# A two-layer diffusion backbone on one core: first norm by VectorE's sum with filling products on TensorE, and a last feed-forward with a late rstd, tokens on partitions and its gate in the weights

## The chip, the core and the metric

The kernel runs on one core of a Trainium2 chip. The core has five engines, each with its own in-order instruction stream: TensorE (PE in the profile, its weight loads PEld), VectorE (DVE), ScalarE (ACT), GpSimd (POOL) and SyncE (SP). SP's stream here holds only DMA issues; its queue is called SPq. Products land in PSUM, which has eight banks of 128 x 512 f32. The metric is device time in microseconds, the median over runs of the whole program. Lower is better.

## The reference

The program computes two layers on 256 latent tokens and 256 context tokens of width 1024. `x` and `ctx` share all weights and have conditioning vectors of their own. Each layer is a feed-forward, a mixer and a second feed-forward, each behind a norm with adaLN (`mx`, `mc`: shift, scale, gate):

```python
mx = jnp.split((cond_x @ mod_w[layer] + mod_b[layer])[:, None, :], N_MOD, axis=-1)
x = x + 0.5 * mx[2] * swiglu(modulate(rms_norm(x, norm_g[layer, 0]), mx[0], mx[1]),
                             ffn_w_in[layer, 0], ffn_w_out[layer, 0])
hx = modulate(rms_norm(x, norm_g[layer, 1]), mx[3], mx[4])
...
x = x + mx[5] * ox
x = x + 0.5 * mx[8] * swiglu(modulate(rms_norm(x, norm_g[layer, 2]), mx[6], mx[7]),
                             ffn_w_in[layer, 1], ffn_w_out[layer, 1])
...
return rms_norm(x, final_norm_g)
```

The mixer that makes `ox` is latent attention in layer 0 and windowed grouped attention in layer 1. The context goes the same way, but not behind the last layer's mixer. `rms_norm(x, g)` is x times the reciprocal root of the mean square of its 1024 values (the rstd), times g; `modulate(h, shift, scale)` is h * (1 + scale) + shift; `swiglu` splits h @ w_in in two halves of 2816, takes silu(first) * second and multiplies by w_out.

## The kernel before

**Layout.** Activations lie with features on the 128 partitions: x is eight tiles (d = 0 to 7) of 128 x 512, the first 256 columns latent tokens (`X`), the rest context (`C`). A matrix product in f32 is made of three products of rounded parts: `split` writes a high half (ScalarE, L182 or L185) and a low half, the rest (VectorE or GpSimd, L183 or L186), and `mm3` (L205) multiplies high by high, high by low and low by high (L210, L211, L212). Weights arrive as 128 x 1024 blocks through `weight` (L194): a load on SP's queue into one of three `wraw` slots, a cast to `whi` and a difference to `wlo`, four slots each.

**Order.** A planner orders each engine's stream by the program's order and by when it takes operands to be ready; `behind(ins)` (L163) puts instructions behind another on its engine. DMAs on SP's queue stay in program order, and an issue that waits for its slot holds all behind it.

**The start.** SP issues four constants, then the eight tiles of x (L76), then for each of the eight feature columns k the adaLN weights of its shift and scale (`load_column`, L114: 1 MB in four loads) and, behind columns 0, 1, 3 and 5, one block of w_in (`lead_weight`, L849). ScalarE squares x (L839), and TensorE sums the squares with a 128 x 128 matrix of ones in plain f32 (L840), which leaves the sum on all partitions; a root and a reciprocal over 128 x 256 follow for each stream (L857, L858). Per column, `mod_on_pe` (L124) multiplies the adaLN weights by the conditioning vectors (L128), copies, transposes (L133) and adds bias and gain per stream on VectorE (L138 to L140); `inputs` (L860) makes the column's scaled, shifted, split input (L863, L865, L866); `lead_products` (L870) multiplies the blocks present so far with the columns present so far.

**Feed-forward.** `ffn` (L410) walks 22 tiles f of 128 hidden features. For each it takes the first product's two halves (`products`, L334: 24 products each), evicts silu(gate) * up as a split pair, and `pump`s (L169) `per_tile` steps of the background. After each of three groups of 8, 7 and 7 tiles, `closing` (L367) multiplies the group by w_out, eight strips of 128 output features, and adds gate times product to x (`residual`, L361). On the last group, `closing` also collects the next norm's squares (`grown`, L266), loads the next sub-layer's first weights (`prefetch`, L310), makes the rstd (`rstd_of`, L217), then the inputs (`stream`, L285), then the first products (`leading`, L317).

**Background.** The other adaLN rows are a matrix-vector product on VectorE: `mod_in_background` (L142) loads eight 128 x 1024 blocks (two `modraw` slots, SP's queue) and adds each into an accumulator per stream (L149, L151), then sums over partitions on TensorE (L157) and transposes.

**The end.** The windowed attention's `closing` leads to the last feed-forward, which has the latent stream alone, so its products are 256 columns wide. Behind it `Final` (L347) scales x by rstd and gain and stores eight strips of features. Its last program lines are:

```python
    sl, nxt = nxt, Sublayer(1, 2, (0,), ffn_specs(1, 1)[:2])
    swa(sl, nxt)
    ffn(nxt, Final(1, 3, (0,), ()))
```

## Time and profile before

| what | us |
|---|---|
| median of 3 runs | 1713.83 (1713.79 to 1716.16) |
| the profiled execution's own time | 1715.96 |
| its span | 1714.2 |
| busy TensorE in the span | 1674.9 (98%) |
| busy VectorE / ScalarE / GpSimd | 1029.5 / 643.9 / 175.2 |
| first 16 us: busy TensorE | 10.07 |
| 16 to 36 us: busy TensorE, granted clock | 15.43, 0.83 |
| 36 to 60 us: busy TensorE | 21.81 |
| 230 to 400 us (inside a feed-forward): busy TensorE | 170.00 |
| 1503 to 1515 us (ahead of the last feed-forward): busy TensorE, granted clock | 7.61, 0.72 |
| 1702.35 to the end: busy TensorE | 1.64 |

How to read the views: a group's row has line, engine, operation, tiles and shapes, count, then busy time and mean ns of one, then idle time of the engine just before and what ended it. A row in order of time begins with start and length in us. A row by stretch has begin and end, length, the busy time of PE, PEld, VectorE, ScalarE and GpSimd with instruction counts, the granted TensorE clock (1.00 is full), the share of the DMA engines and GB/s. Records of matmuls overlap, so the rate of products is read from the distance of their starts, not from a record's length.

### The profile page before, as it was taken

The numbers are of one execution on the slowest core, as the hardware profiler recorded it, in microseconds if no ns is written. First come the engines' busy times: TensorE is split into PE (matmuls) and PEld (weight loads), VectorE is DVE, ScalarE is ACT, GpSimd is POOL, SyncE is SP. The second block draws the span as 40 slices with busy tenths as digits, with TensorE's granted clock in tenths as the row PEclk, the third lists the DMA queues.
The fourth block names the chain that finished last, engine by engine and source line by source line (L and its number), as shares of the span: only waits on it lengthen the run. The fifth ranks groups of instructions, "written<-read, shape, count | busy, mean of one in ns | idle before, by whom it ended". The sixth has DMA issues, their size and how long they took to land.

```text
span 1714.2 us, 23757 instructions
## 1 busy us (share of the span) xinstructions
PE 1674.9 (98%) x9448; PEld 1421.5 (83%) x9448; DVE 1029.5 (60%) x1536; ACT 643.9 (38%) x1087; POOL 175.2 (10%) x173
## 2 busy tenths in 40 slices
PE   7999999999999999999999999999999999989997
PEld 4788888888888898888888898888888897789997
DVE  4877477555568567856857465645433467655554
ACT  4432232224456444213222353223222367554443
POOL 1000000004132040000000130000000352110001
PEclk9999999999999999999999999999999999999998
DMA  9556356442211126644645336734332222145553
GB/s 340 174 192 209 112 198 194 138 132 80 87 50 62 47 68 206 202 158 147 208 145 172 111 111 197 240 117 154 104 101 90 93 90 84 60 149 184 172 188 98
DMA packets 72831, 242.71 MB, mean 142 GB/s; under 512 B 8848, under 2 KB 10640, under 8 KB 72720
## 3 DMA queue, kind: packets, MB, share of 16 engines
q1 hardware_dynamic: 72720, 241.20, 43.1%
q8 instruction: 74, 1.21, 0.3%
q14 instruction: 37, 0.30, 0.1%
HBM read 240.11 MB, written 1.05 MB: 141 GB/s over the span
## 4 chain that ended last, share of the span: by engine, by line
PE 90%; DVE 3%; ACT 3%; DMA 2%; issue 2%; POOL 1%; SPq 0%; POOLq 0%; ACTq 0%; DVEq 0%
PE bank L210 28%; PE bank L211 28%; PE bank L212 28%; DMA r2k<-in_modo 1%; PE bank L157 1%; DVE wlo L183 1%; DVE small L451 0%; PE bank L479 0%; ACT whi L182 0%; PE bank L223 0%; PE bank L102 0%; PE bank L800 0%; ACT tmp L457 0%; DVE r2k L294 0%; DMA big<-in_win 0%
## 5 line engine op out<-in xcount | busy, mean ns | idle before, releaser
L210 PE MATMUL bank<-r2k,whi 128*128 128x512 f32 (+1 forms) x2610 | 916.0, 352 | 4.7 <-ACT r2k L185 2.4
L212 PE MATMUL bank<-r2k,wlo 128*128 128x512 f32 (+1 forms) x2610 | 912.0, 350 | 4.3 <-POOL wlo L183 2.2
L211 PE MATMUL bank<-r2k,whi 128*128 128x512 f32 (+1 forms) x2610 | 913.0, 350 | 2.9 <-DVE r2k L186 1.2
L182 ACT CAST whi<-wraw 128x1024 fp32r<-128x1024 f32 (+1 forms) x313 | 321.6, 1028 | 892.0 <-PE bank L211 537.7
L210 PEld LDWEIGHTS bank<-r2k,whi 128*128 128x128 f32 x2610 | 493.5, 190 | 84.1 <-ACT whi L182 9.2
L212 PEld LDWEIGHTS bank<-r2k,wlo 128*128 128x128 f32 x2610 | 495.1, 190 | 69.7 <-POOL wlo L183 3.1
L211 PEld LDWEIGHTS bank<-r2k,whi 128*128 128x128 f32 x2610 | 495.2, 190 | 68.2 <-DVE r2k L186 1.9
L183 DVE TENSOR_TENSOR wlo<-wraw,whi 128x1024 fp32r<-128x1024 f32 (+1 forms) x302 | 363.6, 1206 | 145.5 <-ACT whi L182 138.8
L151 DVE SCALAR_TENSOR_TENSOR big<-modraw,conds,big 128x1024 f32<-128x1024 f32 x196 | 242.4, 1279 | 12.4 <-DMA modraw<-in_modw 11.9
L248 POOL TENSOR_TENSOR strip<-strip 128x256 f32<-128x256 f32 x64 | 65.7, 1040 | 1319.9 <-issue 657.5
L364 DVE SCALAR_TENSOR_TENSOR x<-bank,mod,x 128x256 f32<-128x256 f32 x192 | 86.1, 480 | 181.9 <-PE bank L212 181.9
L425 DVE TENSOR_TENSOR tmp<-bank,tmp 128x512 f32<-128x512 f32 (+1 forms) x88 | 54.9, 624 | 179.9 <-PE bank L212 178.0
L183 DVE TENSOR_TENSOR r2k<-tmp,r2k 128x512 fp32r<-128x512 f32 (+1 forms) x88 | 54.4, 618 | 1.5 <-ACT r2k L182 1.4
L182 ACT CAST r2k<-tmp 128x512 fp32r<-128x512 f32 (+1 forms) x88 | 49.7, 566 | 10.8 <-DVE tmp L425 10.5
L183 DVE TENSOR_TENSOR r2k<-bank,r2k 128x512 fp32r<-128x512 f32 (+2 forms) x73 | 40.7, 593 | 17.5 <-ACT r2k L182 17.1
L423 ACT ACTIVATE tmp<-bank 128x512 f32<-128x512 f32 (+1 forms) x88 | 47.3, 537 | 7.4 <-PE bank L212 7.4
L451 DVE TENSOR_REDUCE small<-bank 128x1 f32<-128x512 f32 (+1 forms) x64 | 37.0, 614 | 7.4 <-PE bank L774 7.2
L182 ACT CAST r2k<-bank 128x512 fp32r<-128x512 f32 (+2 forms) x73 | 34.4, 524 | 14.2 <-PE bank L212 8.8
L242 ACT ACTIVATE strip<-x 128x256 f32<-128x256 f32 x80 | 30.6, 410 | 17.8 <-DVE x L364 17.0
L186 DVE SCALAR_TENSOR_TENSOR r2k<-r2k,mod 128x256 fp32r<-128x256 f32 x45 | 29.3, 674 | 8.4 <-ACT r2k L185 7.9
L457 ACT ACTIVATE tmp<-bank,small 128x512 f32<-128x512 f32 x32 | 21.8, 687 | 24.8 <-DVE small L453 14.6
L104 DVE TENSOR_TENSOR mod<-bank,c_modb 128x4 f32<-128x4 f32 x56 | 5.3, 154 | 37.2 <-PE bank L102 37.2
(156 smaller groups left out, 933.1 us busy)
## 6 DMA issues: line engine op xcount, KB each, us to landing
wraw<-in_win SPq DMA_DIRECT2D x172, 512.0 KB, 3.5
modraw<-in_modw SPq DMA_DIRECT2D x128, 512.0 KB, 4.2
wraw<-in_wout SPq DMA_DIRECT2D x64, 448.0 KB, 3.3
wraw<-in_wout SPq DMA_DIRECT2D x32, 512.0 KB, 3.8
r2k<-in_modo SPq DMA_DIRECT2D x32, 256.0 KB, 5.8
wraw<-in_mwo SPq DMA_DIRECT2D x8, 512.0 KB, 3.5
wraw<-in_swq SPq DMA_DIRECT2D x8, 512.0 KB, 3.4
wraw<-in_swo SPq DMA_DIRECT2D x8, 512.0 KB, 3.5
```

Source lines behind the costliest of these rows:

```text
L151: nc.vector.scalar_tensor_tensor(acc[s], raw, conds[:, kt, s:s + 1], acc[s], ALU.mult, ALU.add)
L182: nc.scalar.copy(hi, src)
L183: return engine.tensor_tensor(lo, src, hi.bitcast(F32), ALU.subtract)
L210: nc.tensor.matmul(o, lhsT=ah, rhs=bh, start=(i == 0), stop=False)
L211: nc.tensor.matmul(o, lhsT=ah, rhs=bl, start=False, stop=False)
L212: nc.tensor.matmul(o, lhsT=al, rhs=bh, start=False, stop=(i == n - 1))
L242: nc.scalar.activation(q, x, AF.Square)
L248: nc.gpsimd.tensor_tensor(self.parts[0], self.parts[0], q, ALU.add)
L364: nc.vector.scalar_tensor_tensor(xs[d][:, SL[s]], o[:, SL[s]], mod[l][:, s, c:c + 1], xs[d][:, SL[s]], ALU.mult, ALU.add)
L423: nc.scalar.activation(sg[:, :w], og[:, :w], AF.Silu)
L425: nc.vector.tensor_tensor(pr[:, :w], ou[:, :w], sg[:, :w], ALU.mult)
L451: nc.vector.tensor_reduce(top[:, j:j + 1], o[:, :w], axis=AX.X, op=ALU.max)
```

## The change

At the start: the four constants go out on ScalarE's queue, and x comes as four loads of two tiles. The squares are added up on VectorE; four narrow products with a column of ones give the sums by token on partitions, root and reciprocal run over four columns, and four transposes spread the result over partitions again. Column 0's adaLN products come ahead of that in the program. TensorE gets products of ones that nobody reads (`fill`): 40 from the beginning, 3 and 5 behind the first two columns' transposes. The bias and gain steps do both streams in one instruction. The low halves of the four lead weights move from GpSimd to VectorE. In the first feed-forward (`late=2`) the background starts at tile 2, and tiles 12 to 15 take three steps instead of two.

At the end: a class `Raw` takes the place of the last norm. Its first product runs on gain times x, without the rstd, with two more columns that hold the shift; the eviction multiplies by the rstd and adds the shift's product. `last_ffn` makes the second product with tokens on partitions and 512 output features as columns, added up over all 22 tiles in four PSUM banks; the gate (made as a row on all partitions in the background) is multiplied into w_out by GpSimd, and x is added to the sums by products with the identity. The final norm is done from PSUM, and the output is stored token by token. The rest of the program is as before, apart from the layout of x, of w_out and of the output, and a smaller scratch for software DMAs, which the program doesn't use.

```diff
-    cond_raw = load_const("cond", (P, KT, 2))
-    ident = load_const("ident", (P, P))
-    modb = load_const("modb", (P, 2, 72))
-    ng = load_const("ng", (P, 2, 3, KT))
+    cond_raw = load_const("cond", (P, KT, 2), queue=nc.scalar)
+    ident = load_const("ident", (P, P), queue=nc.scalar)
+    modb = load_const("modb", (P, 2, 72), queue=nc.scalar)
+    ng = load_const("ng", (P, 2, 3, KT), queue=nc.scalar)
     x_all = const.tile([P, KT, TT], F32, name="x")
     xs = [x_all[:, d] for d in range(KT)]
-    for d in range(KT):
-        nc.sync.dma_start(xs[d], t["xT"][d])
+    for d in range(0, KT, 2):
+        nc.sync.dma_start(x_all[:, d:d + 2], t["xT"][:, d:d + 2])
...
+    def fill(n, after=None):
+        b = bank()
+        with behind(after):
+            for _ in range(n):
+                nc.tensor.matmul(b[:, :P], lhsT=ones, rhs=ones, start=True, stop=True)
...
+    fill(40)
...
+    def mod_on_pe(k, psA, n=0, after=None):
         sA = tmp()[:, :P]
         nc.scalar.copy(sA, psA[:, :P])
         psB = bank()[:, :P]
-        nc.tensor.transpose(psB, sA, ident)
+        turned = nc.tensor.transpose(psB, sA, ident)
+        if n:
+            fill(n, turned)
         vB = psB.rearrange("p (c i r) -> p c i r", c=2, i=2)
-        for s in range(2):
-            v = mod[0][:, s, :2 * KT].rearrange("p (c k) -> p c k", c=2)[:, :, k]
-            bias = modb[:, 0, :2 * KT].rearrange("p (c k) -> p c k", c=2)[:, :, k]
-            nc.vector.tensor_tensor(v, vB[:, :, 0, s], bias, ALU.add)
-            nc.vector.tensor_tensor(v, vB[:, :, 1, s], v, ALU.add)
-            nc.vector.scalar_tensor_tensor(coefA[0][:, s, 0, k:k + 1], v[:, 1:2], 1.0, ng[:, 0, 0, k:k + 1], ALU.add, ALU.mult)
+        v = mod[0][:, :, :2 * KT].rearrange("p s (c k) -> p c s k", c=2)[:, :, :, k]
+        bias = modb[:, 0, :2 * KT].rearrange("p (c k) -> p c k", c=2)[:, :, k:k + 1].to_broadcast([P, 2, 2])
+        with behind(after):
+            nc.vector.tensor_tensor(v, vB[:, :, 0, 0:2], bias, ALU.add)
+        nc.vector.tensor_tensor(v, vB[:, :, 1, 0:2], v, ALU.add)
+        nc.vector.scalar_tensor_tensor(coefA[0][:, :, 0, k], v[:, 1], 1.0, ng[:, 0, 0, k:k + 1].to_broadcast([P, 2]), ALU.add, ALU.mult)
...
+                n = 0 if f < late else per_tile + (6 * late <= f < 8 * late)
...
+    class Raw(Sublayer):
+        W = T + 2
+        def grown(self, s, d):
+            x = xs[d][:, X]
+            zh, zl = r2k(self.W), r2k(self.W)
+            nc.scalar.activation(zh[:, :T], x, AF.Identity, scale=self.gain(0, d))
+            nc.vector.scalar_tensor_tensor(zl[:, :T], x, self.gain(0, d), zh[:, :T].bitcast(F32), ALU.mult, ALU.subtract)
+            shift = self.shift(0, d).to_broadcast([P, 2])
+            nc.scalar.copy(zh[:, T:], shift)
+            nc.gpsimd.tensor_tensor(zl[:, T:], shift, zh[:, T:].bitcast(F32), ALU.subtract)
+            self.hs.append((zh, zl))
+            self.squares[s].add(x)
+        def terms(self, w, M, cols=None):
+            return [(pair(w, slice(None), slice(k * M, (k + 1) * M)), self.hs[k]) for k in range(KT)]
+        def stream(self, s):
+            pass
+        def leading(self, s):
+            for k in range(KT):
+                for wt, o, M in self.lead:
+                    mm3(o[:M, :self.W], self.terms(wt, M), (k,))
+            _, self.r = self.rstd(s)
...
+        for half in range(2):
+            cols = slice(half * 512, half * 512 + 512)
+            b = bank()
+            nc.tensor.matmul(b, lhsT=ones, rhs=acc[:, cols], start=True, stop=True)
+            nc.vector.tensor_tensor(gate[:, cols], b, gate[:, cols], ALU.add)
+            yield
+        nc.gpsimd.tensor_scalar_mul(gate, gate, 0.5)
...
+        acc = [[bank() for _ in range(2)] for _ in range(2)]
+        r = sl.r
+        held = []
+        def second(f, gu, w):
+            for i in range(2):
+                rows = slice(i * P, (i + 1) * P)
+                for h in range(2):
+                    cols = slice(h * 512, h * 512 + 512)
+                    for j, (a, b) in enumerate(((0, 0), (0, 1), (1, 0))):
+                        nc.tensor.matmul(acc[i][h], lhsT=gu[a][:, rows], rhs=w[b][:, cols],
+                                         start=(f == 0 and j == 0), stop=(f == NF - 1 and j == 2))
+        for f in range(NF):
+            og, ou = next(outs), next(outs)
+            raw = weight_raw(t["woutn"][f])
+            nc.gpsimd.tensor_tensor(raw, raw, gate, ALU.mult)
+            wt = weight_split(raw)
+            while held and f != NF - 2:
+                second(*held.pop(0))
+            ends = small(2)
+            nc.scalar.copy(ends[:, 0:1], og[:, T:T + 1])
+            nc.scalar.copy(ends[:, 1:2], ou[:, T:T + 1])
+            g, u = tmp(T), tmp(T)
+            nc.vector.tensor_tensor(g, og[:, X], r, ALU.mult)
+            nc.scalar.activation(g, g, AF.Silu, bias=ends[:, 0:1])
+            nc.vector.tensor_tensor(u, ou[:, X], r, ALU.mult)
+            nc.vector.scalar_tensor_tensor(u, u, ends[:, 1:2], g, ALU.add, ALU.mult)
+            gu = (r2k(T), r2k(T))
+            hi = nc.scalar.copy(gu[0], u)
+            nc.vector.tensor_tensor(gu[1], u, gu[0].bitcast(F32), ALU.subtract)
+            held.append((f, gu, wt))
+            if f in (5, 7, 9, 11):
+                i, h = (f - 5) // 4, (f - 5) // 2 % 2
+                for d in range(4):
+                    nc.tensor.matmul(acc[i][h][:, d * P:(d + 1) * P], lhsT=xs[4 * h + d][:, i * P:(i + 1) * P], rhs=ident,
+                                     start=False, stop=False)
+        with behind(hi):
+            nc.scalar.activation(small(1), r[:, 0:1], AF.Sqrt)
+        second(*held.pop())
+        for i in range(2):
+            sums, rs = small(2), small(1)
+            ys = [tmp() for _ in range(2)]
+            for h in range(2):
+                nc.scalar.activation(ys[h], acc[i][h], AF.Square, accum_out=sums[:, h:h + 1])
+            nc.vector.tensor_tensor(rs, sums[:, 0:1], sums[:, 1:2], ALU.add)
+            nc.scalar.activation(rs, rs, AF.Sqrt, scale=1.0 / D, bias=eps)
+            nc.vector.reciprocal(rs, rs)
+            for h, queue in enumerate((nc.sync, nc.scalar)):
+                cols = slice(h * 512, h * 512 + 512)
+                if i == 0 and h == 1:
+                    nc.scalar.activation(ys[h], acc[i][h], AF.Copy, scale=rs)
+                    nc.gpsimd.tensor_tensor(ys[h], ys[h], fngr[:, cols], ALU.mult)
+                else:
+                    nc.vector.scalar_tensor_tensor(ys[h], acc[i][h], rs, fngr[:, cols], ALU.mult, ALU.mult)
+                queue.dma_start(out[i, :, cols], ys[h])
...
+        if squares is None:
+            squares = q
+        else:
+            nc.vector.tensor_tensor(squares, squares, q, ALU.add)
     load_table(AF.Sqrt, q)
+    total = bank()
+    for j in range(4):
+        nc.tensor.matmul(total[:, j:j + 1], lhsT=squares[:, j * P:(j + 1) * P], rhs=ones[:, 0:1], start=True, stop=True)
...
+    sums0 = mod_sums(raws[0])
+    root = small()
+    nc.scalar.activation(root, total[:, 0:4], AF.Sqrt, scale=1.0 / D, bias=eps)
+    nc.vector.reciprocal(root, root)
+    wide = bank()
+    for j in range(4):
+        nc.tensor.transpose(wide[:, j * P:(j + 1) * P], root[:, j:j + 1].to_broadcast([P, P]), ident)
+    rstds = [strip() for _ in range(2)]
+    for r, cols in zip(rstds, SL):
+        nc.scalar.copy(r, wide[:, cols])
     def lead_weight(after=None):
         with behind(after):
-            wt = weight_split(wraws[len(sl.lead)], nc.gpsimd)
+            wt = weight_split(wraws[len(sl.lead)])
...
-    mod_on_pe(0, raws[0])
+    mod_on_pe(0, sums0, 3)
     inputs(0)
     for k in range(1, KT + 1):
         if k < KT:
-            mod_on_pe(k, raws[k])
+            mod_on_pe(k, mod_sums(raws[k]), 5 if k == 1 else 0, sl.end if k == 1 else None)
...
-    ffn(sl, nxt, 2)
+    ffn(sl, nxt, 2, 2)
...
-    background.extend(mod_in_background(1, c, (0,)) for c in range(5, 9))
+    background.extend(mod_in_background(1, c, (0,)) for c in range(5, 8))
+    background.append(mod_row_in_background(8))
...
-    sl, nxt = nxt, Sublayer(1, 2, (0,), ffn_specs(1, 1)[:2])
+    sl, nxt = nxt, Raw(1, 2, (0,), ffn_specs(1, 1)[:2])
     swa(sl, nxt)
-    ffn(nxt, Final(1, 3, (0,), ()))
+    last_ffn(nxt)
```

More of the change, by code (lines that the diff above doesn't have):

```diff
@@ L429, in ffn @@
             last = g == len(GROUPS) - 1
-            closing([(t[f"wout{g}"][l, which, d], gu) for d in range(KT)], 2 + 6 * which, l, streams,
+            closing([(t[f"wout{g}"][2 * l + which, d], gu) for d in range(KT)], 2 + 6 * which, l, streams,
                     nxt if last else None, 2 if last else 0, per_tile // 2)
@@ L827, in swa, with products @@
         closing([(t["swo"][d], O) for d in range(KT)], 5, l, (0,), nxt, 0)
+    class Raw(Sublayer):
[19 more added lines that the diff above has]
+            _, self.r = self.rstd(s)
+        def products(self, specs):
+            for i, (ap, size) in enumerate(specs):
+                if i < len(self.lead):
+                    yield self.lead[i][1]
+                else:
+                    wt = weight(ap, size)
+                    o = bank()
+                    mm3(o[:, :self.W], self.terms(wt, P))
+                    yield o
@@ new lines, in mod_row_in_background @@
+    def mod_row_in_background(c):
+        nc.sync.dma_start(gate, t["gater"])
+        acc = big().bitcast(F32)[:, :1024]
+        for kt in range(KT):
+            raw = ring.tile([P, 1024], F32, tag="modraw", name="modraw", bufs=2)
+            nc.sync.dma_start(raw, t["modw"][1, c, kt])
+            if kt == 0:
+                nc.vector.tensor_scalar_mul(acc, raw, conds[:, kt, 0:1])
+            else:
+                nc.vector.scalar_tensor_tensor(acc, raw, conds[:, kt, 0:1], acc, ALU.mult, ALU.add)
+            yield
[4 more added lines that the diff above has]
+            nc.vector.tensor_tensor(gate[:, cols], b, gate[:, cols], ALU.add)
+            yield
+        nc.gpsimd.tensor_scalar_mul(gate, gate, 0.5)
@@ L835, in hybrid_backbone_kernel @@
     sl = Sublayer(0, 0, (0, 1), ffn_specs(0, 0)[:4])
-    total = bank()
+    squares = None
     for d in range(KT):
@@ L1005 @@
     got = r.results[0]["out_x"]
[L1006 removed]
+    return np.ascontiguousarray(got.reshape(1, T, D))
```

56 lines of the change are left out of this document (24 added, 32 removed).

## The prediction

> **What bounds the kernel now.** I read the page's engine shares first, then the busy time by stretch, then the order of time inside the two stretches in which TensorE is not full.
>
> ```profile
> span 1714.2 us, 23757 instructions
> PE 1674.9 (98%) x9448; PEld 1421.5 (83%) x9448; DVE 1029.5 (60%) x1536; ACT 643.9 (38%) x1087; POOL 175.2 (10%) x173
> ```
>
> ```profile
> 16.00:36.00 20.00, 15.43 (x190) 10.44 (x191) 13.01 (x43) 8.84 (x18) 5.50 (x3) 0.83 1.05 402
> 36.00:60.00 24.00, 21.81 (x174) 15.61 (x172) 15.33 (x45) 7.80 (x16) 3.94 (x2) 1.00 0.41 141
> ...
> 1503.00:1515.00 12.00, 7.61 (x44) 7.03 (x43) 7.41 (x13) 8.06 (x17) 4.99 (x7) 0.72 0.27 89
> 1516.60:1702.35 185.75, 185.67 (x1543) 185.06 (x1542) 104.02 (x131) 82.04 (x116) 6.04 (x6) 1.00 0.52 168
> 1702.35:1714.20 11.85, 1.64 (x11) 1.07 (x9) 3.78 (x7) 3.95 (x8) 2.31 (x3) 0.61 0.25 89
> ```
>
> Columns: stretch, length, busy PE, PEld, DVE, ACT, POOL (with instructions), granted clock, DMA share, GB/s. TensorE bounds the span, so time is to be had only where it idles, runs at a low clock, or does work that can go. The change touches such places: the first 60 us, the 13.7 us ahead of the last feed-forward's steady part, that part (185.75 us, full), and the 11.85 us behind its last product.
>
> The start, in order of time (start, length, engine, line):
>
> ```profile
> 2.58 3.75 SPq L76 DMA_DIRECT2D x<-in_xT  x8
> 5.93 10.05 PE L840 MATMUL bank<-tmp,ones 128*128 128x512 f32 x16 [5.93 <-ACT tmp L839]
> 8.17 3.99 ACT L839 ACTIVATE tmp<-x 128x512 f32<-128x512 f32 x6 [1.25 <-DMA x<-in_xT]
> 16.52 3.37 DVE L858 RECIPROCAL strip<-strip 128x256 f32<-128x256 f32 x2 [12.94 <-ACT strip L857]
> 20.34 0.48 DVE L863 SCALAR_TENSOR_TENSOR strip<-x,coefA,strip 128x256 f32<-128x256 f32 x1
> 24.79 1.94 PE L128 MATMUL bank<-r2k,cond 128*32 128x128 f32 x32
> 26.66 0.80 PE L210 MATMUL bank<-r2k,whi 128*128 128x512 f32 x1
> 30.08 1.08 PE L128 MATMUL bank<-r2k,cond 128*32 128x128 f32 x32
> 34.09 1.04 ACT L182 CAST whi<-big 128x1024 fp32r<-128x1024 f32 x1
> 35.20 2.37 POOL L183 TENSOR_TENSOR wlo<-big,whi 128x1024 fp32r<-128x1024 f32 x1 [8.50 <-DMA r2k<-in_modo]
> 36.26 1.33 DVE L140 SCALAR_TENSOR_TENSOR coefA<-mod,c_ng 128x1 f32<-128x1 f32 x1
> 38.03 0.15 DVE L140 SCALAR_TENSOR_TENSOR coefA<-mod,c_ng 128x1 f32<-128x1 f32 x1
> 45.28 2.36 POOL L183 TENSOR_TENSOR wlo<-big,whi 128x1024 fp32r<-128x1024 f32 x1 [7.70 <-ACT whi L182]
> 48.03 0.39 PE L210 MATMUL bank<-r2k,whi 128*128 128x512 f32 x1
> 52.14 0.39 PE L212 MATMUL bank<-r2k,wlo 128*128 128x512 f32 x1
> 58.40 2.48 DVE L151 SCALAR_TENSOR_TENSOR big<-modraw,conds,big 128x1024 f32<-128x1024 f32 x2
> 60.79 1.22 DVE L183 TENSOR_TENSOR wlo<-wraw,whi 128x1024 fp32r<-128x1024 f32 x1
> 62.07 0.50 PE L212 MATMUL bank<-r2k,wlo 128*128 128x512 f32 x1 [1.97 <-DVE wlo L183]
> ```
>
> The reciprocal over 128x256 twice holds the first input back to 20.34. TensorE then runs cold (0.80 at 26.66 for a product that takes 0.39 at 48.03), and each of the four lead weights waits for a cast behind the inputs and 2.36 us of GpSimd. After the leads it stands idle for 1.97 us until 62.07, because a weight's low half queues on VectorE behind two adaLN steps (58.40 to 60.88).
>
> The last feed-forward:
>
> ```profile
> 1502.89 0.28 PE L212 MATMUL bank<-r2k,wlo 128*128 128x256 f32 x1
> 1516.54 0.28 PE L211 MATMUL bank<-r2k,whi 128*128 128x256 f32 x1
> 1702.07 0.28 PE L212 MATMUL bank<-r2k,wlo 128*128 128x256 f32 x1
> 1710.85 1.02 SPq L359 DMA_DIRECT2D out_x<-strip  x2
> ```
>
> **The start, worked out.** Constants leave SP's queue, so x starts about 1.8 us earlier (2.58 to 0.74 at best) and the loads behind it as much; the last square ends at 10.3 instead of 12.16. Seven adds on VectorE follow at 618 ns each (row below), the last about 11.1. The forty filling products are plain f32 of 128 columns: the 16 L840 records took 10.05 us for 8 products of 512, mostly cold, so 40 of a quarter the width cost at most 12.5 us and end between 10 and 13; I take 12.6. Then the four sums and column 0's adaLN products (1.1), square root and reciprocal over four columns (0.4 together), four transposes, two copies (0.4 each): rstd near 15.3 and the first input at 15.7, 4.6 us earlier than 20.34. The clock then stays up: the adaLN products at 24.79 take 1.08 for 1.94 (-0.9), and the nine products between 26.66 and 30.08 take 9 x 0.228 = 2.05 for 3.4 (-1.35); 0.228 is 4.11 us over the 18 products from 48.03 to 52.14. So the third weight's cast moves from 34.09 to about 27.3 (-6.8). Its low half costs 1.22 on VectorE instead of 2.37 (-1.1), the fourth's again (-1.1), and TensorE finds less high-half work to do meanwhile (+0.5): the leads end 8.5 us earlier. Behind them no adaLN step is issued for two tiles, SP does not stand on their loads, and the stall to 62.07 shrinks to about 0.1: -1.9. Sum -10.4. The adaLN steps come back as a third one per tile in tiles 12 to 15. There VectorE has 3 x 2 x 1.28 for them (L151's mean on the page) plus 2.44 for two weights and 1.3 for products and split, 11.4 us in a tile of 48 x 0.228 = 10.9: 2 us too much over four tiles, inside what three weights ahead cover; I charge +0.5, 3 if the cover is gone, and +0.3 for the gate row's wider sums on TensorE. Bounds of the start: -3 (the earlier loads and one shorter low half) to -13 (TensorE's own work, 96 x 0.228 + 8 x 1.1 + 1.8 of filling, without a gap from 13 us).
>
> ```profile
> L183 DVE TENSOR_TENSOR r2k<-tmp,r2k 128x512 fp32r<-128x512 f32 (+1 forms) x88 | 54.4, 618 | 1.5 <-ACT r2k L182 1.4
> L151 DVE SCALAR_TENSOR_TENSOR big<-modraw,conds,big 128x1024 f32<-128x1024 f32 x196 | 242.4, 1279 | 12.4 <-DMA modraw<-in_modw 11.9
> ```
>
> [...]
>
> **The last feed-forward, worked out.** These rows price its parts (mean ns in the middle):
>
> ```profile
> L183 DVE TENSOR_TENSOR wlo<-wraw,whi 128x1024 fp32r<-128x1024 f32 x49 | 60.0, 1225 | 40.2 <-ACT whi L182 40.2
> L182 ACT CAST whi<-wraw 128x1024 fp32r<-128x1024 f32 x49 | 51.4, 1049 | 75.3 <-PE bank L211 37.6 <-issue 35.4 <-PE bank L212 1.5
> L425 DVE TENSOR_TENSOR tmp<-bank,tmp 128x256 f32<-128x256 f32 x22 | 9.3, 424 | 16.0 <-PE bank L212 15.6 <-ACT tmp L423 0.5
> ...
> L457 ACT ACTIVATE tmp<-bank,small 128x512 f32<-128x512 f32 x32 | 21.8, 687 | 24.8 <-DVE small L453 14.6
> wraw<-in_win SPq DMA_DIRECT2D x37, 512.0 KB, 3.5
> 1390.87 1.02 PE L739 MATMUL bank<-tmp,permr 128*128 128x256 f32 x4
> 1391.73 1.03 PE L739 MATMUL bank<-r2k,permr 128*128 128x256 f32 x4
> ```
>
> Before, from 1503.0 (end of the attention's products): 13.7 us to the steady part at 1516.6, 185.75 us of 1536 products (0.1209 each), 11.85 us of tail: 211.2. After: the 48 lead products need no rstd, so they follow at once, the first 42 covering the last strip's residual, gain and split: 48 x 0.121 = 5.8. Sums and transposes of the rstd still pass TensorE: 1.2. The other 1008 products have 258 columns; between 0.1209 at 256 and 0.228 at 512 a straight line gives 0.1217: 122.7 us (bounds 121.9 and, at the price of 512, 230). The second product is 264 of 512 instead of 528 of 256: 60.2 us for 63.8. The residual enters as 16 plain f32 products of 128 columns: two of 256 took 0.86 us at L739, so 0.215 each, 3.4; unhidden weight loads could make it 9; I take 3.8. Waits at entry and in the last two tiles, where two second products are kept back to cover the last eviction: 1. The tail: four squares at 0.69 and some 0.2 for the accumulated sum, the first two under the last products; then add, root, reciprocal (0.6), two scalings from PSUM (0.7 each), and a DMA like the last before (issue 1710.85, end 1714.2: 3.3 for two): about 7. Sum 201.7, that is -9.5 (bounds -13 and, waits of 0.3 a tile and a 9 us residual, +2).
>
> Per tile TensorE needs 48 x 0.1217 + 12 x 0.228 = 8.6 us. VectorE has 3 x 1.225 + 4 x 0.42 = 5.4, ScalarE about 4.3, GpSimd the gating of one weight, 2.36 by the rows of the low halves. None is the bound, but the gated weight's way round its slot is long: 3.5 load + 2.36 + 1.05 + 1.23 + handovers 0.4 = 8.5. It is used a tile and a half after its cast, which covers delays. The new gains and splits in the attention's closing (about half a microsecond a strip on ScalarE and on VectorE, beside a cast and a low half, against 24 x 0.12 = 2.9 us of products) are hidden there.
>
> The row at 36.26 speaks against the gating: a 128x1 step, 0.15 at 38.03, lasted 1.33 until GpSimd's 2.37 had ended. [...]
>
> **Sum.** -10.4 + 0.8 - 9.5 = -19.1. The profiled execution took 1715.96 with a span of 1714.2, so 1696.9 in its terms; it stands 2.1 above the median of 1713.83, so the median should be about 1695.
>
> **Rivals.**
> *Only the end gains.* The start stays tied to the columns' loads, which run at 402 GB/s from 16 to 36 us, and VectorE, now with 4 x 1.22 of low halves among its inputs, is late for each weight: -3 there, 1703. For it: DMA share 1.05. Against: from 36 us the share falls to 0.41 and TensorE still has 24 us to go.
> *The start reaches TensorE's floor*, the planner filling gaps: -13 there, 1692 with the rest, 1689 if the tail is shorter too. Against: the order of weights, each behind inputs 1, 3, 5.
> *The gated weight sets the pace.* If GpSimd and VectorE block each other by one operation each (+1.2), the slot's round is 9.7; it exceeds 8.6 by 1.1, over 21 tiles 23 us less a cover of 12: +11, 1706.
> *Slower.* One mechanism: that round grows to 11 us, VectorE's two SBUF inputs waiting 2.4 for the gating and GpSimd's 1.2 for them in every tile. Then (11 - 8.6) x 21 - 12 = +38: 1733. It decides from a round of 10.1 on, where 31 - 12 eats the 19 gained. For it: 36.26. Against: slots and casts run ahead of need by more than a tile.
> *It does not do what it says:* 258 columns fall out of the fast rate. At the price of 512 that is +108: 1803. No row has such a width; a straight line is likelier.
>
> **How the numbers follow.** Forecast 0.56 (own range 1689 to 1701), only the end 0.13, the floor 0.11, the paced end 0.10, slower 0.06, slow width 0.02, a return to the old time 0.02. Eight in ten lie from 1686 to 1711. About 0.2% (3.4 us) is what a measurement here tells from no change. Faster: 0.56 + 0.13 + 0.11 + 0.10 = 0.90; same 0.02; slower 0.08.
>
> **What would show it.** Right: first input near 16, clock full from 16 to 36, leads ended 8 us earlier, no stall behind them, lead products of the last feed-forward dense from the attention's last one on, tiles of 8.6 us, tail near 7. Wrong: low halves of the leads later than 30 and 39; waits of TensorE on low halves or gated weights in every tile; the 258-wide product above 0.125 apart; filling still running after 14 us.

## The result and the profile after

| | median us | ratio to the kernel before | 95% interval |
|---|---|---|---|
| before, in the same rounds | 1714.38 (1713.79 to 1716.16) | 1 | |
| after | 1700.76 (1699.09 to 1701.59) | 0.9916 | 0.9904 to 0.9929 |

The change made the kernel 13.6 us faster; 19.1 were forecast. The profiled execution of after took 1699.09 us with a span of 1697.3, 16.9 less than the span before. The other 3.3 us of the difference to 13.6 come from the two profiled executions: that of before stood 1.6 above its median, that of after 1.7 below. The run without gating further down had one execution at a granted clock of 0.752 (2062.65 us), which its figures leave out.

The shares of after, and busy time by stretch (columns as in the prediction: length, busy PE, PEld, DVE, ACT, POOL, granted clock, DMA share, GB/s):

```profile
PE 1672.6 (99%) x9294; PEld 1417.5 (84%) x9294; DVE 1080.8 (64%) x1538; ACT 645.4 (38%) x1132; POOL 222.5 (13%) x186
```

```profile
16.00:36.00 20.00, 18.51 (x214) 12.97 (x209) 14.07 (x35) 8.16 (x18) 0.00 (x0) 1.00 1.04 384
36.00:60.00 24.00, 24.00 (x160) 18.48 (x159) 15.42 (x32) 12.61 (x21) 0.00 (x0) 1.00 0.58 200
...
1490.76:1496.56 5.80, 5.80 (x50) 5.80 (x49) 2.61 (x5) 3.53 (x6) 2.84 (x4) 1.00 0.79 244
1496.56:1509.88 13.32, 10.20 (x72) 9.13 (x71) 10.02 (x13) 7.55 (x15) 4.31 (x2) 1.00 0.53 161
1509.88:1666.67 156.79, 156.79 (x1114) 147.92 (x1112) 128.05 (x123) 70.21 (x123) 49.74 (x17) 1.00 0.54 173
1666.67:1682.06 15.39, 13.58 (x98) 13.17 (x96) 12.76 (x12) 6.65 (x13) 5.58 (x2) 0.89 0.37 122
1682.06:1690.30 8.24, 8.24 (x38) 6.57 (x36) 2.31 (x6) 4.33 (x11) 0.00 (x0) 1.00 0.01 2
1690.30:1697.30 7.00, 0.12 (x1) 0.00 (x0) 2.56 (x6) 1.73 (x7) 1.27 (x1) 0.88 0.40 150
```

TensorE now works through 16 to 60 us almost without a gap, at full clock. In the last feed-forward it follows the attention at once (5.80 us of lead products), then loses time in the entry, is full for 156.79 us, and loses time again in a place that the prediction charged almost nothing for: the 15.39 us from 1666.67, at a clock of 0.89. The entry's products need 0.95 for the rstd, 48 x 0.12 and 12 x 0.229, together 9.5 of its 13.32 us: 3.8 lost. The 96 of the last two tiles need 11.5 of 15.39: 3.9 lost. The tail behind the last product is 7.0 us.

The start of after, in order of time (start, length, engine, line):

```profile
1.03 11.58 PE L88 MATMUL bank<-ones 128*128 128x128 f32 x80 [1.03 <-DVE ones L79]
13.33 1.08 PE L143 MATMUL bank<-r2k,cond 128*32 128x128 f32 x32
15.85 0.88 DVE L999 SCALAR_TENSOR_TENSOR strip<-x,coefA,strip 128x256 f32<-128x256 f32 x2
28.71 1.03 ACT L198 CAST whi<-big 128x1024 fp32r<-128x1024 f32 x1
38.02 1.03 ACT L198 CAST whi<-big 128x1024 fp32r<-128x1024 f32 x1
52.49 0.50 PE L228 MATMUL bank<-r2k,wlo 128*128 128x512 f32 x1
```

The last row answers 62.07 before: the first low-half product behind the leads, 9.6 us earlier and without its stall of 1.97.

Where the 16.9 us of span lie, by three marks of the traces: the first load of the query weights of the sliding-window attention is issued at 1331.7 for 1342.4, so start and middle gave 10.7; from there the attention's last product ends 159.1 us later (1490.76) for 160.8 (1503.21), 1.7; and from there to the end of the program it is 206.5 for 211.0, 4.5.

### The profile page after: what moved, and what is told of

Same layout as the page of the kernel before. It is cut to its first block, busy times and chain, and to the rows that moved or that the text cites. A ratio compares the mean times of both kernels' runs of the same rounds, so it can differ in the third digit from the quotient of the medians.

```text
span 1697.3 us, 23433 instructions
## 1 busy us (share of the span) xinstructions
PE 1672.6 (99%) x9294; PEld 1417.5 (84%) x9294; DVE 1080.8 (64%) x1538; ACT 645.4 (38%) x1132; POOL 222.5 (13%) x186
## 4 chain that ended last, share of the span: by engine, by line
PE 79%; DMA 5%; DVE 5%; ACT 4%; POOL 3%; issue 2%; ACTq 0%; DVEq 0%; SPq 0%; POOLq 0%
PE bank L226 25%; PE bank L227 25%; PE bank L228 24%; DMA wraw<-in_woutn 4%; POOL wraw L912 3%; DVE wlo L199 2%; ACT whi L198 2%; DMA r2k<-in_modo 1%; PE bank L177 1%; DVE big L171 1%; PE bank L239 1%; DVE small L454 0%; PE bank L482 0%; PE bank L906 0%; DMA modraw<-in_modw 0%
## 5 line engine op out<-in xcount | busy, mean ns | idle before, releaser
L226 PE MATMUL bank<-r2k,whi 128*128 128x512 f32 (+2 forms) x2434 | 866.7, 357 | 0.9 <-ACT small L918 0.9
L227 PE MATMUL bank<-r2k,whi 128*128 128x512 f32 (+2 forms) x2434 | 861.9, 354 | 2.6 <-DVE r2k L202 1.2
L228 PE MATMUL bank<-r2k,wlo 128*128 128x512 f32 (+2 forms) x2434 | 861.4, 354 | 1.1 <-DVE wlo L199 0.9
L226 PEld LDWEIGHTS bank<-r2k,whi 128*128 128x128 f32 x2434 | 459.1, 189 | 79.5 <-ACT whi L198 9.2
L227 PEld LDWEIGHTS bank<-r2k,whi 128*128 128x128 f32 x2434 | 460.2, 189 | 68.4 <-DVE r2k L202 1.9
L171 DVE SCALAR_TENSOR_TENSOR big<-modraw,conds,big 128x1024 f32<-128x1024 f32 x189 | 233.3, 1278 | 14.7 <-DMA modraw<-in_modw 14.4
L428 DVE TENSOR_TENSOR tmp<-bank,tmp 128x512 f32<-128x512 f32 x66 | 45.6, 690 | 160.7 <-PE bank L228 158.1
L912 POOL TENSOR_TENSOR wraw<-wraw,gate 128x1024 f32<-128x1024 f32 x22 | 63.5, 2888 | 127.2 <-DMA wraw<-in_woutn 127.0
L906 PE MATMUL bank<-whi,r2k 128*128 128x512 f32 x176 | 58.0, 392 | 3.1 <-DVE r2k L927 1.8
L927 DVE TENSOR_TENSOR r2k<-tmp,r2k 128x256 fp32r<-128x256 f32 x22 | 51.0, 2318 | 0.9 <-ACT r2k L926 0.9
L199 DVE TENSOR_TENSOR r2k<-tmp,r2k 128x512 fp32r<-128x512 f32 x66 | 45.1, 684 | 1.4 <-ACT r2k L198 1.4
L198 ACT CAST r2k<-tmp 128x512 fp32r<-128x512 f32 x66 | 41.0, 622 | 12.8 <-DVE tmp L428 12.4
L426 ACT ACTIVATE tmp<-bank 128x512 f32<-128x512 f32 x66 | 38.9, 590 | 3.7 <-PE bank L228 3.7
```

What stands on the lines that cost most here:

```text
L171: nc.vector.scalar_tensor_tensor(acc[s], raw, conds[:, kt, s:s + 1], acc[s], ALU.mult, ALU.add)
L198: nc.scalar.copy(hi, src)
L199: return engine.tensor_tensor(lo, src, hi.bitcast(F32), ALU.subtract)
L226: nc.tensor.matmul(o, lhsT=ah, rhs=bh, start=(i == 0), stop=False)
L227: nc.tensor.matmul(o, lhsT=ah, rhs=bl, start=False, stop=False)
L228: nc.tensor.matmul(o, lhsT=al, rhs=bh, start=False, stop=(i == n - 1))
```

## The experiments

Each was timed in five rounds, in three sessions; the median of before was 1715.5, 1715.4 and 1715.2 there. Differences are therefore taken between ratios, times 1714.4. The interval of one ratio is 1.8 to 2.8 us to either side, so that of a difference of two is about 3 to 3.5 (an estimate that takes them as independent). A difference below that is told only by the traces, where they show the same place directly. All kernels that keep the changed start execute the same code ahead of it, yet in their traces the lead products of the last feed-forward end between 1494.8 and 1498.3; so spans are compared from there on. Those scatter too: six traces with the last feed-forward of after (after itself, the end alone and the four runs on the start's terms) take 205.3 to 207.8 us from the attention's last product to the end.

### What costs 7.7 us in the last feed-forward

From the timeline of after: two issues of the gated weight's load, one later round of it, TensorE's two stops in the last tile (in brackets, how long an engine stood and for whom), and the stretch behind the second stop:

```profile
1540.27 0.33 SPq L207 DMA_DIRECT2D wraw<-in_woutn  x1
1549.13 0.33 SPq L207 DMA_DIRECT2D wraw<-in_woutn  x1
...
1664.87 0.33 SPq L207 DMA_DIRECT2D wraw<-in_woutn  x1
1668.53 2.84 POOL L912 TENSOR_TENSOR wraw<-wraw,gate 128x1024 f32<-128x1024 f32 x1 [6.02 <-DMA wraw<-in_woutn]
1671.40 1.99 ACT L198 CAST whi<-wraw 128x1024 fp32r<-128x1024 f32 x2 [3.08 <-POOL wraw L912]
1672.48 2.36 DVE L199 TENSOR_TENSOR wlo<-wraw,whi 128x1024 fp32r<-128x1024 f32 x2 [0.83 <-ACT whi L198]
1673.73 0.33 SPq L207 DMA_DIRECT2D wraw<-in_woutn  x1
...
1673.44 0.39 PE L226 MATMUL bank<-r2k,whi 128*128 128x258 f32 x1 [0.86 <-ACT small L918]
1674.89 0.39 PE L228 MATMUL bank<-r2k,wlo 128*128 128x258 f32 x1 [0.95 <-DVE wlo L199]
```

```profile
1675.00:1678.50 3.50, 3.50 (x18) 3.50 (x18) 2.84 (x5) 1.91 (x4) 1.04 (x1) 0.53 0.42 136
```

Three weights a tile and three raw buffers: the gated weight always gets the same buffer, and its round (load 3.66, gating 2.84, cast, low half, the next load's issue) is 8.87 us, while TensorE's tile is 8.50. ScalarE takes the gated weight's cast first, so the next input weight's cast stands behind it for 3.08 us. TensorE's two gaps are 1.14 and 1.22 us from product to product for 0.12, 2.1 lost, and the 3.5 us behind them pass at a clock of 0.53, 1.75 lost.

The stops stand in all six traces with this last feed-forward, the half clock in four. In the runs with adaLN steps from the first tile on and with the constants on SP's queue (both below) the clock stays at 1.00 behind the same two stops, and the last two tiles take 14.1 and 14.2 us for 15.39. This is the second:

```profile
1669.99:1684.15 14.16, 12.30 (x97) 11.72 (x96) 12.05 (x11) 6.11 (x12) 5.82 (x2) 1.00 0.37 131
```

So 2.6 of the 3.9 us come with the stops alone, and about 1.2 depends on the execution.

I called the round that is too long the pace theory. Its rival, the slot theory, blamed the two second products that are kept back in the last two tiles and hold split-weight buffers. At the entry the port theory (a name only: what the two engines share, no trace shows) blamed GpSimd's gating for a VectorE subtraction that took 2.59 instead of 0.43:

```profile
1504.64 3.41 POOL L912 TENSOR_TENSOR wraw<-wraw,gate 128x1024 f32<-128x1024 f32 x1 [7.19 <-DMA wraw<-in_woutn]
1505.75 2.59 DVE L927 TENSOR_TENSOR r2k<-tmp,r2k 128x256 fp32r<-128x256 f32 x1
1508.39 1.20 PE L906 MATMUL bank<-whi,r2k 128*128 128x512 f32 x4 [1.80 <-DVE r2k L927]
1509.73 0.43 DVE L927 TENSOR_TENSOR r2k<-tmp,r2k 128x256 fp32r<-128x256 f32 x1 [0.47 <-ACT r2k L926]
```

**Nothing kept back.**

```diff
-            while held and f != NF - 2:
+            while held:
```

> The changed kernel with one condition less: a tile's second product is always issued one tile later, also in the last two tiles, where the changed kernel keeps two of them back. Pace theory (the gated weight goes round one and the same slot of three in 8.87 us, by its loads' issues at 1540.27, 1549.13 and 1558.01, while TensorE needs 8.50 us a tile, so the stock of weights runs out at the end): the last tile's products are asked for 2.75 us later, which is more than the 2.1 us for which TensorE stood at 1672.5 and 1673.7, so these go, and with them the half clock of 3.5 us behind them (about 1.75): -3.9; then the last second product waits for the last eviction, 2.9 us less 2.75 of cover plus handover: +0.5. Sum 1697.4 us for the 1700.8 of the changed kernel. Slot theory (the two products kept back hold two of the four split-weight slots): the same gain, so this run alone does not tell the two apart. If the clock stays down for another reason: 1700 to 1701.

Measured: 1697.43 us, ratio 0.9900 (0.9883 to 0.9916), 2.7 less than the changed kernel; from the lead products' end 198.4 for 200.7. The stops and the half clock behind them are gone (14.26 us at clock 1.00 for the last two tiles' input products and the second product between them), and a new stop stands ahead of the last second product, longer than expected:

```profile
1666.91:1681.17 14.26, 14.26 (x110) 13.77 (x109) 12.05 (x11) 6.21 (x12) 5.77 (x2) 1.00 0.39 134
1681.17:1688.10 6.93, 5.75 (x26) 4.17 (x24) 3.05 (x6) 4.32 (x12) 0.00 (x0) 1.00 0.01 2
```

```profile
1685.25 0.50 PE L906 MATMUL bank<-whi,r2k 128*128 128x512 f32 x1 [1.18 <-ACT r2k L926]
```

So keeping products back saves 1.2 to 1.4 us at the end, and goes with a loss of 2.6 to 3.9 here only because weights are late.

**Own buffers for the gated weight.**

```diff
-            raw = weight_raw(t["woutn"][f])
+            raw = weight_raw(t["woutn"][f], 1024, big().bitcast(F32))
```

(and the final gain's row is loaded at f == NF - 2 instead of first)

> The changed kernel with the last output weight loaded into the four large buffers, which are free by then, instead of always the same one of the three weight buffers; the gating stays on GpSimd; the final gain's row is loaded in the last tiles. Pace theory: no slot comes round every tile any more, weights run ahead, and the 3.9 us in the last two tiles go while two second products are still kept back: 1696.9 us; the 1.8 us at the entry stay. Slot theory (the split-weight slots held by the kept-back products): nothing changes, 1700.8. Port theory alone: nothing changes, low halves still 2.3 us.

Measured: 1695.39 us, ratio 0.9887 (0.9872 to 0.9902), 5.0 less than the changed kernel; from the lead products' end 196.8 for 200.7, the 3.9 expected (1.2 of it is the half clock of after's trace). The last two tiles' input products are dense, while two second products are still kept back, and the entry is unchanged to the hundredth (13.32):

```profile
1498.34:1511.66 13.32, 10.20 (x73) 9.12 (x72) 10.03 (x13) 7.55 (x15) 2.89 (x1) 1.00 0.46 159
1668.44:1679.96 11.52, 11.52 (x98) 11.51 (x97) 7.05 (x10) 5.25 (x10) 0.00 (x0) 1.00 0.00 1
```

This decides for the pace theory and against the slot theory.

**No gating.** The product with the gate is left out.

```diff
-            nc.gpsimd.tensor_tensor(raw, raw, gate, ALU.mult)
```

> The changed kernel without the multiplication of the last output weight by the gate (this leaves that part of the computation out; the gate row is still summed). It prices the gating as a whole. Pace and port theory together: round 8.87 - 2.9 = 6.0 us, no GpSimd beside VectorE: 3.9 and 1.8 go, 1695.1 us, and about 1.6 of waiting at the entry stay, behind the activation-table load (1.28 at 1501.69) and the casts. Slot theory: 1699. If the gating costs nothing on the path: 1700.8.

Measured: 1693.14 us, ratio 0.9874 (0.9858 to 0.9891), 7.2 less; from the lead products' end 194.7 for 200.7, 6.0 where 5.7 were expected. Both places gain at once, 2.1 at the entry and 3.9 at the end:

```profile
1494.79:1506.02 11.23, 9.91 (x73) 9.21 (x71) 7.94 (x13) 7.55 (x15) 0.00 (x0) 1.00 0.49 165
1662.80:1674.32 11.52, 11.52 (x98) 11.51 (x96) 7.05 (x10) 5.30 (x10) 0.00 (x0) 1.00 0.27 91
```

**Gating on VectorE.**

```diff
-            nc.gpsimd.tensor_tensor(raw, raw, gate, ALU.mult)
+            nc.vector.tensor_tensor(raw, raw, gate, ALU.mult)
```

> The changed kernel with the gating of the last output weight on VectorE instead of GpSimd. Pace theory: the round of the gated weight becomes 8.87 - 2.9 + 1.25 = 7.2 us, under the tile's 8.50, so the stall in the last two tiles (3.9 with its half clock) goes. Port theory (a VectorE operation on two SBUF inputs stands while GpSimd gates: 2.318 us mean for 0.42): the 1.8 us for which the first second product waited go too: 1700.8 - 3.9 - 1.8 = 1695.1 us, and the low half of the gated activation takes 0.42 everywhere. Slot theory (two kept-back products hold split-weight slots): only the 1.8 go: 1699. Against both: VectorE, 6.7 us of 8.5 busy, stands for the gated weight's load with the evictions behind it: 1701 or more.

Measured: 1699.97 us, ratio 0.9912 (0.9897 to 0.9927), no difference; from the lead products' end 200.8. The port part came as expected (entry 11.40 us for 13.32), but the round did not shrink to 7.2:

```profile
1659.86 0.33 SPq L207 DMA_DIRECT2D wraw<-in_woutn  x1
1664.71 1.22 DVE L912 TENSOR_TENSOR wraw<-wraw,gate 128x1024 f32<-128x1024 f32 x1 [3.03 <-DMA wraw<-in_woutn]
1667.71 1.22 DVE L199 TENSOR_TENSOR wlo<-wraw,whi 128x1024 fp32r<-128x1024 f32 x1
1668.96 0.33 SPq L207 DMA_DIRECT2D wraw<-in_woutn  x1
```

It is 9.10 us here, and between 8.5 and 9.4 from the fourth tile on: the gating starts 4.85 after the issue instead of 3.66, and the low half stands in VectorE's queue behind three other steps. VectorE waits 3.03 us in front of it with the evictions behind. The last two tiles' products took 16.82 us there. A shorter operation did not make a shorter round, because the round passes the queue of the engine that got it.

### The two halves of the change

**Start alone.** The kernel before with the changed start; edits outside the last feed-forward as in the change.

```diff
-    sl, nxt = nxt, Raw(1, 2, (0,), ffn_specs(1, 1)[:2])
+    sl, nxt = nxt, Sublayer(1, 2, (0,), ffn_specs(1, 1)[:2])
     swa(sl, nxt)
-    last_ffn(nxt)
+    ffn(nxt, Final(1, 3, (0,), ()))
```

> The kernel before with the changed start alone (constants off SP's queue, sums on VectorE, filling products, lead low halves on VectorE, adaLN steps held back for two tiles); its last feed-forward is the old one. The traces put the start and the middle at 10.7 us earlier (end of the third feed-forward) and the sliding-window attention at 1.5 more. If the 1.5 comes with the start (or is the spread of the start from run to run): 1714.4 - 12.2 = 1702.2 us and an attention of the old length less 1.5. If it comes with the last feed-forward's part: 1703.7. The prediction's own terms give -10.4 + 0.5 = 1704.5. The rival by which the start is tied to the columns' loads gives -3: 1711.

Measured: 1702.82 us, ratio 0.9928 (0.9914 to 0.9943), 12.3 less than before. The mark of the attention's first load lies at 1331.7, as after; the attention is 1.6 us shorter, as after, and the rest 211.0 us long, as before.

**End alone.** The kernel before with the same two lines the other way round.

> The kernel before with the changed last feed-forward alone (raw products first, tokens on partitions, gate in the output weight, the gate's row in the background); its start is the old one. From the traces, last attention product to end of program: 211.0 before, 206.3 after, so -4.7: 1709.7 us if the attention keeps its old length, 1708.2 if its 1.5 us comes with this part. The prediction's own term was -9.5: 1704.9. The same stall as in the changed kernel is expected in the last two tiles, since the gated weight's round has nothing to do with the start.

Measured: 1711.24 us, ratio 0.9976 (0.9966 to 0.9987), 4.1 less than before. The attention keeps its length (160.7), and from its last product to the end it is 207.8 us, with the same two stops (1.36 and 0.94) in the last tile. Its mark at the attention lies at 1340.6, 1.7 ahead of that of before, though the code up to there differs only in the gate's row in the background: so much a single trace can err on the start.

The two together make 16.4, after has 14.4 by its ratio: equal within their intervals. The prediction's -9.6 for the start was 1 to 3 us too small, and its -9.5 for the end twice too large.

**The 1.6 us in the attention** belong to neither half's work. In the attention's last heads TensorE stands 2.5 us for ScalarE in every kernel, and then the clock falls to 0.79 in some executions and stays at 1.00 in others. Before, after, and with own buffers (stretch from the end of that stop to the closing's first product):

```profile
1471.60:1479.90 8.30, 8.30 (x49) 5.29 (x49) 2.61 (x6) 2.67 (x5) 0.00 (x0) 0.79 0.01 2
```

```profile
1460.96:1467.63 6.67, 6.67 (x48) 4.60 (x48) 2.63 (x6) 2.70 (x5) 0.00 (x0) 1.00 0.01 2
```

```profile
1461.12:1469.40 8.28, 8.28 (x48) 5.29 (x48) 2.63 (x6) 2.69 (x5) 0.00 (x0) 0.79 0.01 2
```

The third has the same code there as the second, and the same stop, but 1.6 us more at a clock of 0.79; the start alone and no gating had it at 1.00, the end alone at 0.79, and of all 14 traces 8 have the long stretch (8.2 to 8.3 us) and 6 the short one (6.7). So the 1.6 us are part of the spread of an execution, not of the change. What decides between the two, no trace shows.

### The start's terms

**Lead low halves on GpSimd again.**

```diff
-            wt = weight_split(wraws[len(sl.lead)])
+            wt = weight_split(wraws[len(sl.lead)], nc.gpsimd)
```

> The changed kernel with the low halves of the four lead weights on GpSimd again. Prediction's term: 2.37 instead of 1.22 us for the third and again for the fourth weight, so the fourth weight's cast and the leads' end come 2.2 us later: fourth cast at 40 instead of 37.5 to 38.7, time 1703. Loads theory (the columns' landing sets the pace from 13 to 36 us, the low halves wait for nobody): fourth cast unchanged, 1700.8. Port theory on top (VectorE stands while GpSimd makes a low half, as at 36.26 in the kernel before): more than 2.2.

Measured: 1703.78 us (1701.72 to 1708.12), ratio 0.9938 (0.9926 to 0.9950), 3.8 more than the changed kernel. Its profiled execution was its slowest, and there the second column landed late (TensorE waited 2.49 us for it), so 44.24 for the fourth cast is an upper end:

```profile
16.00:36.00 20.00, 15.63 (x164) 10.60 (x165) 9.25 (x24) 6.51 (x15) 5.20 (x3) 0.83 1.02 375
...
26.18 1.47 DVE L160 SCALAR_TENSOR_TENSOR coefA<-mod,c_ng 128x2 f32<-128x2 f32 x1
27.69 0.73 PE L228 MATMUL bank<-r2k,wlo 128*128 128x512 f32 x2 [1.48 <-POOL wlo L199]
44.24 1.03 ACT L198 CAST whi<-big 128x1024 fp32r<-128x1024 f32 x1
```

The term was 2.2, which 3.8 with about 3 us to either side does not exclude. The rows show what it left out: VectorE's 128x2 step takes 1.47 us beside GpSimd's 2.35 from 25.28 on, for 0.16 in after, and the granted clock from 16 to 36 us is 0.83 for 1.00.

**adaLN steps from the first tile on.**

```diff
-    ffn(sl, nxt, 2, 2)
+    ffn(sl, nxt, 2)
```

> The changed kernel with two adaLN steps in each of the first feed-forward's tiles from its first one on, as in the kernel before, instead of none in two tiles and three in four later ones. Prediction's terms: the stall behind the leads comes back (+1.9), the late background's +0.5 goes: 1702.2 us, and TensorE waits about 2 us for a low half on VectorE some 10 us earlier than the 62.07 of the kernel before. Rival: with the leads 9.6 us earlier and their low halves on VectorE the steps find another place, and nothing changes: 1700.8.

Measured: 1705.48 us, ratio 0.9940 (0.9927 to 0.9952), 4.1 more by the ratio, where 1.4 were expected; an interval of about 3 us to either side of the difference reaches down to that. The five executions lie in two groups, 1701.9 and 1702.0, and 1705.5 to 1707.5. In the profiled one, the slowest, the stall behind the leads came back twice:

```profile
56.03 0.80 PE L228 MATMUL bank<-r2k,wlo 128*128 128x512 f32 x1 [2.51 <-DVE wlo L199]
71.30 0.50 PE L228 MATMUL bank<-r2k,wlo 128*128 128x512 f32 x1 [2.15 <-DVE wlo L199]
```

The first product behind the first stall also ran cold (0.80, against 0.50 behind the second).

**Constants on SP's queue again, and no filling.** Two runs that both make the first input late.

```diff
-    cond_raw = load_const("cond", (P, KT, 2), queue=nc.scalar)
+    cond_raw = load_const("cond", (P, KT, 2))
```

(and so for ident, modb and ng)

> The changed kernel with the four constants on SP's queue ahead of x again. Prediction's term: all loads behind them come 1.8 us later, so the first input comes 1.8 later, if the filling's end at 12.6 does not cover a part; the columns land 1.8 later and with them the fourth cast (39.3 to 40.5) and everything behind: 1702.6 us. If TensorE's own work sets the start: 1701.

```diff
-    fill(40)
...
-        if n:
-            fill(n, turned)
```

> The changed kernel without the 58 filling products. Clock theory: TensorE comes cold to the first adaLN products, the granted clock of 16 to 36 us falls from 1.00 towards the 0.83 of the kernel before, which costs the 0.9 + 1.35 us that the prediction booked, while the sums for the norm, which stood behind the filling until 12.45, come about 1 us sooner: +1.2, 1702.0 us. Loads theory (from 13 to 36 us the DMA engines are full at 384 GB/s, and TensorE waits for the columns): the clock falls but the time stays within 0.5 of 1700.8.

Measured: 1700.66 us, ratio 0.9917 (0.9904 to 0.9931), with the constants back; 1700.89 us, ratio 0.9919 (0.9906 to 0.9932), without filling. Neither is different from the changed kernel. The first input with the constants back; then, without filling, two rows in order of time and one by stretch:

```profile
18.88 0.88 DVE L999 SCALAR_TENSOR_TENSOR strip<-x,coefA,strip 128x256 f32<-128x256 f32 x2
```

```profile
18.61 1.94 PE L142 MATMUL bank<-r2k,cond 128*32 128x128 f32 x32
19.38 0.88 DVE L996 SCALAR_TENSOR_TENSOR strip<-x,coefA,strip 128x256 f32<-128x256 f32 x2
16.00:36.00 20.00, 18.20 (x177) 11.88 (x173) 12.88 (x37) 7.85 (x19) 0.00 (x0) 1.00 1.04 385
```

The first input comes 3.0 and 3.5 us later than after, the fourth cast (40.09 and 40.75 for 38.02) 2.1 and 2.7, and the mark at the sliding-window attention 1.5 in both (1333.2). That a late first input is made up for by half on the way agrees with the full DMA share (1.04) from 16 to 36 us, but a gain of 1 to 2 us from either edit is not excluded by these times. Both traces also have the long stretch in the attention (8.2 us each).

Without filling, 32 adaLN products still take 1.94 us at 18.61, where after needs 1.08 at 13.33. So the filling does warm TensorE up, but no gain in time from it is shown. The granted clock from 16 to 36 us reads 1.00 all the same: here that column does not show a cold start.

The start alone gained 12.3 us. The low halves (3.8) and the late background (4.1) are its only terms that a run shows; no run took out the new path of the norm or the joint bias steps, so what the rest is made of stays open.

### A faster version

**Own buffers, and one gating on VectorE,** the one that meets the first low half of the entry.

```diff
-            nc.gpsimd.tensor_tensor(raw, raw, gate, ALU.mult)
+            (nc.vector if f == 5 else nc.gpsimd).tensor_tensor(raw, raw, gate, ALU.mult)
```

> The version with the output weight in the four large buffers (own slots), and the gating of the sixth tile's output weight on VectorE, because that is the one which GpSimd does just while VectorE makes the first gated low half (2.58 us at 1507.52 in the run with own slots, 0.42 alone). Port theory: the first second product waits 0.3 instead of 1.8, so 1695.4 - 1.5 = 1693.9 us; against it the 1.23 us of gating stand in VectorE's queue ahead of that low half: in the worst case nothing is gained, 1695.4.

Measured: 1693.96 us, ratio 0.9879 (0.9863 to 0.9895), 6.3 less than the changed kernel and 20.7 less than before. Own buffers alone had 5.0 of it; the other 1.4 cannot be told from nothing by these times, but the trace has 195.6 for 196.8 from the lead products' end, and the cause in its rows. The low half takes 0.42 again and the first second product waits 0.16 for it:

```profile
1505.21 0.42 DVE L928 TENSOR_TENSOR r2k<-tmp,r2k 128x256 fp32r<-128x256 f32 x1
1505.69 0.74 PE L904 MATMUL bank<-whi,r2k 128*128 128x512 f32 x2 [0.16 <-DVE r2k L928]
```

**The Silu table behind the square root** in addition.

```diff
-        nc.scalar.activation(r, b[:, 0:2], AF.Sqrt, scale=1.0 / dim, bias=eps)
+        nc.scalar.activation(r, b[:, 0:2], AF.Sqrt, scale=1.0 / dim, bias=eps); soon and load_table(soon, r)
```

(and this norm hands in AF.Silu as `soon`)

> The best version so far (output weight in the large buffers, the sixth tile's gating on VectorE, 1694.0 us), with the Silu table loaded right behind the last feed-forward's square root instead of behind a cast (its load took 1.28 at 1501.69 and 1503.47, just ahead of the first Silu). Entry theory: the first Silu starts 1.1 us sooner and the 1.32 us that the first second product waited go: 1692.8. Against it the casts and the transposes' copy stand behind the table load and the low halves with them: 1694 or up to 0.5 later.

Measured: 1695.30 us, ratio 0.9883 (0.9870 to 0.9897), no gain; from the lead products' end 195.2 for the 195.6 of the version before it. TensorE still waits at the same place:

```profile
1506.44 0.50 PE L904 MATMUL bank<-whi,r2k 128*128 128x512 f32 x1 [1.53 <-ACT r2k L927]
```

The first Silu came 6.7 us behind the lead products' end instead of 6.4: the table load left the one place in ScalarE's queue and pushed a cast and the rstd's copy back by as much. That this wait is the table's was wrong; what else in that queue sets it stays open.

## Why the prediction was right, and where it was wrong

The direction held, and 1700.76 lies inside the forecast's own range of 1689 to 1701, at its upper end, 5.8 above the middle. That it still lies inside is in part luck: the start gained 1 to 3 us more than forecast and hides some of the 5 that the end lacks. By its steps:

- **Start, -10.4 + 0.8.** Measured -10.7 in the traces, -12.3 (0.9928) by the time of the start alone, which includes the attention's 1.6. Filling's end 12.6 (12.61 here, 11.7 to 13.2 over the other runs, as its cold part, 5.1 us here, lasts 3.2 to 6.1, so the close hit is luck), first input 15.7 (15.85), clock 1.00 from 16 to 36: as forecast. But that clock reads 1.00 without filling as well, with the same time, so the 2.25 us (0.9 and 1.35) that were booked for a warm clock are not shown. The third cast was 1.4 us later than the 27.3 forecast, of which TensorE's four stops for columns (0.26, 0.44, 0.27 and 0.17) are 1.1; no stall is left behind the leads. The rival of a start tied to the loads (-3) fell. Of the single terms, the low halves' 2.2 measured 3.8 and the background's 1.4 measured 4.1, each with an interval that reaches the forecast; the profiled executions lose clock with the stalls (0.83 from 16 to 36 us in the one, 0.93 from 36 to 60 in the other), which the terms leave out. The terms for the first input look oversized: 3 us there are 1.5 at the attention's mark, and nothing in the time.
- **End, -9.5.** Measured -4.5 in after, -4.1 alone. Residual 3.75 (3.8), tail 7.0 (7), rstd 0.95 (1.2), lead products 5.80 (5.8) held. A product of 258 columns takes 0.120, not 0.1217, which gave 1.7 and ended the slow-width rival. The step that failed is one term: "Waits at entry and in the last two tiles ...: 1". It measured 3.8 at the entry and 3.9 in the last two tiles (2.6 where the clock stayed up). With it the sum comes out: 201.7 - 1 + 7.7 - 1.7 - 0.25 = 206.45, measured 206.5. The sentence "None is the bound" was the reason: it weighed each engine's load against 8.6, and the gated weight's round of 8.5 against the same number, and found both below. The round was 8.87 and the tile 8.50.
- **The rival of the paced end** had the mechanism, with a round of 9.7 and +11 against the forecast. Its cover was right in kind: the stock lasted until the last tile. Its size was not: 0.37 us a tile come to some 8 us over 21 tiles, less than the 12 that the rival took as cover, and yet 2.1 us of stops were left, so the cover was 6 at most (an estimate). The half clock of the next 3.5 us added 1.75 in this trace. The prediction did not count any clock loss behind a stop.
- **The port.** The prediction held the row at 36.26 against the gating, but weighed each engine by its load and called none the bound. That was right for the load and missed the latency: the row group below has a mean of 2.318 us for an operation that takes 0.42 where GpSimd does not gate, and one of them lies on TensorE's path at the entry. Which steps are hit the traces show: beside the gating from 1516.09 to 1518.49 in after, L923, with one input from a PSUM bank, took its 0.42 us, and L924, with both inputs from tiles outside PSUM (in SBUF), 2.21 for 0.48; beside GpSimd's 35.20 to 37.57 in before, L139, with one input from a bank, took 0.16 at 36.06, and L140, with both from SBUF, the 1.33 at 36.26.

```profile
L912 POOL TENSOR_TENSOR wraw<-wraw,gate 128x1024 f32<-128x1024 f32 x22 | 63.5, 2888 | 127.2 <-DMA wraw<-in_woutn 127.0
L927 DVE TENSOR_TENSOR r2k<-tmp,r2k 128x256 fp32r<-128x256 f32 x22 | 51.0, 2318 | 0.9 <-ACT r2k L926 0.9
```

## What to carry to other kernels

Count a buffer's round (issue, load, every operation with its queue, release) against the period of its consumer, not only each engine's load: with as many buffers as loads in a period, one kind of tile gets the same buffer every time, and a round 0.4 us over the period shows only at the end, when the stock is gone. With stops of TensorE of some two microseconds count the lower clock that can follow: here 3.5 us at 0.53 or 8.3 us at 0.79, 1.2 to 1.6 us more in the executions where it did. Moving an operation to an engine where it is shorter does not shorten the round if it then stands in a fuller queue: here 1.22 us for 2.84, and a round of 9.10 for 8.87.
